# Differential attention scores: crosswise stacked queries for the mixed products and 64-row pairs for the high-by-high products

## The chip, the cores and the metric

The kernel runs on one core of one Trainium2 chip. The metric is the device time of one execution in microseconds. Before the change it is 1485.94 us, the median of three runs (1484.71 to 1486.96).

## What is computed

A trunk of two layers over 1024 tokens of width 1024. Layer 0 is a differential attention: eight heads, each with two components of 64 query and key columns, whose two softmax maps are subtracted before they meet the values. Layer 1 is a latent attention (MLA), which the change doesn't touch. Cut to the part of layer 0:

```python
q = _rope(q.reshape(b, s, 2 * DA_HEADS, DA_QK_DIM), positions)   # 16 x 64
k = _rope(k.reshape(b, s, 2 * DA_HEADS, DA_QK_DIM), positions)
...
def block(qb):
    sc = jnp.einsum('bqhcd,bkhcd->bhcqk', qb, k, preferred_element_type=f32) * scale
    p = jax.nn.softmax(sc, axis=-1)
    p = p[:, :, 0] - lam * p[:, :, 1]
    return jnp.einsum('bhqk,bkhd->bqhd', p.astype(v.dtype), v)
```

All inputs are float32, and the result has to be near float32.

## The kernel before

**Products in two parts.** A float32 matrix is kept as a high part of type fp32r (rounded by a copy) and a low part (the rest). A projection is then three products, high by high, low by high, high by low (`mm3`, lines 173 to 175).

**Scores of layer 0.** A head's two components have 64 columns each, so a stack of high over low part fills the 128 rows of TensorE. `stack_k` (line 295) builds for each half of 512 keys a tile `ks` of 2 x 512 columns: component 0 has high in rows 0 to 63 and low in rows 64 to 127, component 1 has high in rows 64 to 127 and low in rows 0 to 63. `stack_q` (line 302) builds two tiles for each half of 512 queries: `qa` has the high part in both row halves, `qb` the low part in both. It takes two casts on ScalarE, two subtractions on GpSimd and four copies from one row half to the other by SyncE's DMA queue. A query tile of 128 then needs, for each component, `qa` and `qb` against the two key halves: four products of 128 rows and 512 columns, which give all four of high and low by high and low.

**A query tile** (`attn0`, from line 821). Eight heads have eight tiles of 128 queries. For each tile `scores(0)` fills one score bank (128 x 1024 in PSUM; there are two such banks), `softmax_part` takes its maximum on VectorE (L352) and its exponential on ScalarE (L354) into `e` in SBUF, `scores(1)` does the same with the second bank, where the exponential stays in place. VectorE's reciprocal (L864), a scale (L865) and L866 subtract the second map from the first, and L866 is the last to read the second bank.

**What lies between.** Behind a tile come the tails of the two tiles before it: `turn` transposes `e` by four products of 128 columns (L335), ScalarE casts them into `pth` (L337), VectorE makes `ptl` (L338); `pv` multiplies them with the values, 12 products of 256 columns at a time, and only in every second tile (an odd one, `t` = 1). `fill(i)` takes the next steps of `stream0`, the q, k and z projections of the next head, three products of 512 columns to a step; tables (`FILL0`, `FILL7` for the last head) say how many steps at each of six places.

**What sets the order.** The code states the work in the order given above; the framework's scheduler then orders each engine's instructions by its own estimate, so neighbours in the code needn't stay neighbours. Every engine runs its instructions in the order in which they stand, and waits by semaphores.

Of the kernel before, what the change touches and what calls it, by code (L numbers as in the profile page):

```python
# [11 lines left out]
F32 = mybir.dt.float32  # L12
F32R = mybir.dt.float32r
# [8 lines left out]
P = 128  # L22
D = 1024
T = 1024
NT = T // P
KT = D // P
HF = 512
# [9 lines left out]
    NVEC += _c  # L37
DEF = 9
DEF1 = 0
FILL0 = ((1, 2, 1, 1, 1, 0), (1, 1, 1, 1, 1, 1))  # L40
FILL1 = ((1, 0, 1, 0), (0, 1, 0, 0)) * 4
SPL1 = 2
Z_PRE = 8
# [5 lines left out]
OP1 = (12, 4)  # L49
LAST = [(((0, 1, 2, 3), 0, HF),), (((0, 1), 0, HF), ((2,), 0, HF), ((3,), 0, 256), ((3,), 256, HF))]  # L50
Z_LAST = 2
FILL7 = ((0, 1, 1, 1, 1, 1),) * 4
G_WAIT = 3
G1_AT = 7
VB = (2, 4)
# [18 lines left out]
def f32v(ap):  # L74
    return ap.bitcast(F32)
# [3 lines left out]
def trunk(ctx: ExitStack, tc: tile.TileContext, A, out):  # L79
    nc = tc.nc  # L80
    SP, PE, V, S, G = nc.sync, nc.tensor, nc.vector, nc.scalar, nc.gpsimd
# [220 lines left out]
    def stack_q(qa, qb, r):  # L302

        S.copy(qa[0:64, 0, :], r[0:64])
        S.copy(qa[64:128, 1, :], r[64:128])
        G.tensor_sub(qb[0:64, 0, :], r[0:64], f32v(qa[0:64, 0, :]))
        G.tensor_sub(qb[64:128, 1, :], r[64:128], f32v(qa[64:128, 1, :]))
        for t in (qa, qb):
            SP.dma_start(f32v(t[64:128, 0, :]), f32v(t[0:64, 0, :]))
            SP.dma_start(f32v(t[0:64, 1, :]), f32v(t[64:128, 1, :]))  # L310

    def store_v(l, sp, acc, tt, fh):
        v = sp.tile([P, 2, HF], F32R, name="v_hl", tag="vst", bufs=VB[l])
        S.copy(v[:, 0, :], acc)
        V.tensor_sub(v[:, 1, :], acc, f32v(v[:, 0, :]))  # L315
# [33 lines left out]
    def softmax_part(ap_, s_ps, zs):  # L349

        nm = sm.tile([P, 1], F32, name="nm")
        V.reduce_max(nm, s_ps, axis=AX.X, negate=True)  # L352
        e = ap_.tile([P, T], F32, name="e", tag="e", bufs=3) if ap_ else s_ps
        S.activation(e, s_ps, AF.Exp, bias=nm, scale=1.0, accum_out=zs)  # L354
        return e

    def bcast_rows(sp, y, tag, bufs):
# [258 lines left out]
    KS, QS, GZ = {}, {}, {}  # L616
# [13 lines left out]
    def q_done(h):  # L630
        def f(acc, half):
            fin = rope(wp, acc, half, SC0)

            def g():
                qa = a0a.tile([P, 2, HF], F32R, name="qa", tag="qs", bufs=4)
                qb = a0a.tile([P, 2, HF], F32R, name="qb", tag="qs", bufs=4)
                stack_q(qa, qb, fin())
                QS.setdefault(h, [None, None])[half] = qa, qb

            side.add(*[None] * DEF, g)  # L640
        return f
# [34 lines left out]
    a0a = pool(st2a, "a0a")  # L676
# [29 lines left out]
    a0b = pool(st2b, "a0b")  # L706
# [80 lines left out]
    tails, hooks = [None, None], []  # L787
# [16 lines left out]
    def after_scores(fill, n):  # L804

        prev, last = tails
        if last:
            last.turn(0)
        fill(n)
        if prev:  # L810
            prev.pv(0)
        fill(n + 1)
        new = hooks[:]
        if prev:
            prev.pv(1)
        fill(n + 2)
        for f in new:
            hooks.remove(f)
            f()

    def attn0(h, fills, extra=None, late=None):

        def close(half, o_, zz):
            if late and half == 1:
                ctx_["late"] = late(o_, zz)
                return
            o = a0b.tile([P, HF], F32, name="o", tag="o", bufs=2)
            sq = a0b.tile([P, HF], F32, name="osq", tag="osq", bufs=4)
            head_out(o_, o, sq)
            subln(o, sq, zz, half, h, None)  # L830

        ctx_ = dict(pool=a0b, l=0, h=h, open=lambda half: None, close=close)
        for qp in range(4):
            half = qp // 2
            if qp % 2 == 0:
                zz = sm.tile([P, 4], F32, name="zz")
            for t in range(2):
                ti = (qp * 2 + t) % 4
                ql = slice(ti * P, (ti + 1) * P)
                zs = [zz[:, ti : ti + 1], sm.tile([P, 1], F32, name="z1")]  # L840
                es = []
                fl = fills(qp * 2 + t)

                def fill(i):
                    if fl[i]:
                        stream0.step(fl[i])

                def scores(c):
                    s_ps = bank("sc", "s", [P, T])
                    qa, qb = QS[h][half]  # L850
                    for src, fst in ((qa, True), (qb, False)):
                        for kc in range(2):
                            PE.matmul(s_ps[:, kc * HF : (kc + 1) * HF], src[:, c, ql], KS[h][kc][:, c, :], start=fst, stop=not fst)  # L853
# [10 lines left out]
                V.reciprocal(z1, z1)  # L864
                V.tensor_scalar(z1, z1, z0, neglam[:, 0:1], op0=ALU.mult, op1=ALU.mult)  # L865
                V.scalar_tensor_tensor(out=e0, in0=e1, scalar=z1[:, 0:1], in1=e0, op0=ALU.mult, op1=ALU.add)  # L866
                fill(2)
                after_scores(fill, 3)
# [12 lines left out]
    def load_ot(l, dst, src):  # L881
# [580 lines left out]
```

## Time and profile before

| what | value |
|---|---|
| median of three runs | 1485.94 us |
| profiled execution | 1489.61 us |
| its span | 1487.8 us |
| mean granted TensorE clock | 0.986 |
| TensorE products (PE) | 7424, all in the form 128*128 |
| maxima of 128 x 1024 (L352), both layers | 192, 1219 ns each |
| transposes (L335), both layers | 1024, 275 ns each, overlapping |

The profiled execution is 3.7 us above the median, so a sum made on it is carried over to the median as a difference. A product's duration in the profile runs from its start to its modelled end and overlaps with the next, so what a stream of them costs is read from start to start. "PE" is the product, "PEld" the load of its weights. In a row of waits the three numbers are the total in us, how often, and the longest.

### The profile page before, as it was taken

What the parts mean: (1) busy time and instruction counts of PE and PEld (TensorE: products, weight loads), DVE (VectorE), ACT (ScalarE), POOL (GpSimd) and SP (SyncE); (2) the same over time, 40 slices, a digit from 0 to 9 for tenths busy, and PEclk for the clock granted to TensorE, in tenths of its full rate; (3) what the DMA queues carried; (4) which work ended last, traced back from release to release, by engine and by line L of the source; (5) the groups of instructions that cost most, each with busy time, mean ns of one, the idle gap of its engine ahead of it and who ended that gap; (6) DMA issues with size and microseconds to landing.
All of it is one profiled execution on the core that took longest, in us unless ns stands there. A gap on an engine that the chain in (4) does not pass through costs nothing.

```text
span 1487.8 us, 20422 instructions
## 1 busy us (share of the span) xinstructions
PE 1411.2 (95%) x7424; PEld 1173.4 (79%) x7424; DVE 863.0 (58%) x1294; ACT 707.0 (48%) x1248; POOL 608.2 (41%) x472
## 2 busy tenths in 40 slices
PE   4999799999999999998899999999999999999997
PEld 3777688888888888877787778777888888888885
DVE  7655767776676767677435535224545555555455
ACT  4432365656565655666343332124445454455442
POOL 3426163636454544545561254213122041233582
PEclk9999899999999999998999999999999999999998
DMA  8885923233332323243453126467223232252453
GB/s 270 268 244 166 307 58 92 79 92 79 89 83 86 79 82 94 67 136 112 164 176 120 43 61 198 137 178 218 74 67 95 66 116 62 62 180 80 156 164 140
DMA packets 119829, 187.46 MB, mean 126 GB/s; under 512 B 17328, under 2 KB 54320, under 8 KB 119728
## 3 DMA queue, kind: packets, MB, share of 16 engines
q1 hardware_dynamic: 119728, 186.16, 41.7%
q8 instruction: 58, 0.95, 0.3%
q14 instruction: 43, 0.35, 0.1%
HBM read 124.82 MB, written 37.70 MB: 109 GB/s over the span
## 4 chain that ended last, share of the span: by engine, by line
PE 68%; DMA 13%; DVE 7%; POOL 5%; issue 3%; ACT 3%; SPq 2%; POOLq 0%; ACTq 0%; DVEq 0%
PE s L1284 9%; PE acc L175 8%; PE acc L174 8%; PE acc L173 8%; PE s L853 8%; PE tr L335 7%; PE pv L174 4%; PE pv L173 4%; PE pv L175 4%; DMA vS<-v_hl 3%; PE oacc L175 2%; PE oacc L174 2%; PE oacc L173 2%; DMA wor<-in_w_out 1%; POOL wol L911 1%
## 5 line engine op out<-in xcount | busy, mean ns | idle before, releaser
L352 DVE TENSOR_REDUCE nm<-s 128x1 f32<-128x1024 f32 x192 | 233.8, 1219 | 72.4 <-PE s L853 65.5
L337 ACT CAST pth<-tr 128x512 fp32r<-128x512 f32 x256 | 150.4, 587 | 255.0 <-PE tr L335 253.6
L338 DVE TENSOR_TENSOR ptl<-tr,pth 128x512 fp32r<-128x512 f32 x256 | 176.2, 688 | 151.5 <-ACT pth L337 150.3
L200 POOL TENSOR_TENSOR wl<-wraw,wh 128x512 fp32r<-128x512 f32 (+2 forms) x94 | 116.2, 1238 | 276.8 <-ACT wh L199 244.0
L335 PE MATMUL tr<-ident,e 128*128 128x128 f32 x1024 | 156.0, 275 | 4.0 <-DVE ptl L338 3.6
L335 PEld LDWEIGHTS tr<-ident,e 128*128 128x128 f32 x1024 | 121.9, 141 | 46.0 <-DVE ptl L338 17.6
L354 ACT ACTIVATE e<-s,nm 128x1024 f32<-128x1024 f32 x128 | 143.4, 1120 | 22.2 <-DVE nm L352 21.6
L173 PE MATMUL acc<-h0h,wh 128*128 128x512 f32 x360 | 149.6, 416 | 1.5 <-DVE v_hl L315 1.5
L173 PE MATMUL pv<-pth,vt 128*128 128x256 f32 x512 | 147.9, 289 | 1.4 <-ACT pth L337 1.4
L174 PE MATMUL pv<-ptl,vt 128*128 128x256 f32 x512 | 146.7, 286 | 0.0
L175 PE MATMUL pv<-pth,vt 128*128 128x256 f32 x512 | 145.9, 285 | 0.0
L175 PE MATMUL acc<-h0h,wl 128*128 128x512 f32 x360 | 142.5, 396 | 0.9 <-POOL wl L200 0.9
L174 PE MATMUL acc<-h0l,wh 128*128 128x512 f32 x360 | 142.1, 395 | 0.0
L911 POOL TENSOR_TENSOR wol<-wor,woh 128x512 fp32r<-128x512 f32 x64 | 86.2, 1366 | 75.2 <-ACT woh L910 74.8
L173 PEld LDWEIGHTS pv<-pth,vt 128*128 128x128 f32 x512 | 98.7, 193 | 5.2 <-ACT pth L337 2.4
L174 PEld LDWEIGHTS pv<-ptl,vt 128*128 128x128 f32 x512 | 98.6, 193 | 2.9
L175 PEld LDWEIGHTS pv<-pth,vt 128*128 128x128 f32 x512 | 98.6, 193 | 0.0
L853 PE MATMUL s<-ks,qa 128*128 128x512 f32 x256 | 85.6, 417 | 13.4 <-ACT e L354 5.7
L716 POOL TENSOR_TENSOR o<-o,bc_s 128x512 f32<-128x512 f32 x30 | 46.5, 1549 | 121.2 <-DVE o L1254 94.6
L199 ACT CAST wh<-wraw 128x512 fp32r<-128x512 f32 (+2 forms) x94 | 55.2, 589 | 84.1 <-PE acc L174 39.2
L287 POOL TENSOR_TENSOR rp_sw<-rp_sw,sinT 128x512 f32<-128x512 f32 x42 | 55.0, 1309 | 76.2 <-DMA rp_sw<-rp_raw 53.4
L866 DVE SCALAR_TENSOR_TENSOR e<-s,z,e 128x1024 f32<-128x1024 f32 x64 | 82.0, 1281 | 1.5
(491 smaller groups left out, 3300.9 us busy)
## 6 DMA issues: line engine op xcount, KB each, us to landing
wraw<-in_w_s SPq DMA_DIRECT2D x76, 256.0 KB, 2.9
ada<-in_ada_ss SPq DMA_DIRECT2D x32, 512.0 KB, 5.0
vS<-v_hl SPq DMA_DIRECT2D x32, 512.0 KB, 5.5
vt<-vS SPq DMA_DIRECT2D x32, 512.0 KB, 3.7
wor<-in_w_out SPq DMA_DIRECT2D x64, 256.0 KB, 3.5
rp_sw<-rp_raw SPq DMA_DIRECT2D x168, 64.0 KB, 2.0
bc_s<-bc_d SPq DMA_DIRECT2D x34, 256.0 KB, 3.7
ada<-in_ada_g SPq DMA_DIRECT2D x16, 512.0 KB, 5.3
```

The costliest lines, as they stand in the source:

```text
L173: PE.matmul(psum, ah, bh, start=first, stop=False)
L174: PE.matmul(psum, ah, bl, start=False, stop=False)
L175: PE.matmul(psum, al, bh, start=False, stop=last)
L200: (V if pair_of else G).tensor_sub(l_[:, :n], raw[:, :n], f32v(h_[:, :n]))
L335: PE.transpose(tr[:, j, :], p[:, kt * P : (kt + 1) * P], ident)
L337: S.copy(pth[kh][:, :, dst], tr)
L338: V.tensor_sub(ptl[kh][:, :, dst], tr, f32v(pth[kh][:, :, dst]))
L352: V.reduce_max(nm, s_ps, axis=AX.X, negate=True)
L354: S.activation(e, s_ps, AF.Exp, bias=nm, scale=1.0, accum_out=zs)
L853: PE.matmul(s_ps[:, kc * HF : (kc + 1) * HF], src[:, c, ql], KS[h][kc][:, c, :], start=fst, stop=not fst)
L911: G.tensor_sub(lo, raw, f32v(hi))
L1284: PE.matmul(s_ps[:, kc * HF : (kc + 1) * HF], lhs, rhs(kc), start=i == 0, stop=i == 4)
```

## The change

The mixed terms and the high-by-high terms are separated. `stack_x` replaces `stack_q`: one cast makes `qn`, the high part of both components as they lie (component 0 in rows 0 to 63, component 1 in rows 64 to 127); `qx` has crosswise, for component 0, the low part in rows 0 to 63 and the high part in rows 64 to 127, and for component 1 the high part in rows 0 to 63 and the low part in rows 64 to 127. A product of `qx` with `ks` over 128 rows is low by high plus high by low. The high-by-high term is a product of `qn` and `ks` over the 64 rows of its component. Low by low is no longer computed. A query tile has two products of 128 rows and two of 64 rows for each component, eight in all as before. SyncE makes two copies per query half where it made four. Both score banks are now filled together: the four mixed products, then the four of 64 rows, alternating between the components, and only then the two softmax parts. The places of the fills and the two tables are arranged anew, with 12 steps for two tiles of `FILL0` and 5 for a tile of `FILL7` as before.

```diff
-FILL0 = ((1, 2, 1, 1, 1, 0), (1, 1, 1, 1, 1, 1))
+FILL0 = ((1, 2, 1, 1, 1, 0), (1, 2, 1, 1, 1, 0))
...
-FILL7 = ((0, 1, 1, 1, 1, 1),) * 4
+FILL7 = ((1, 1, 1, 1, 1, 0),) * 4
...
+    def stack_x(qn, qx, r):
+
+        S.copy(qn, r)
+        G.tensor_sub(qx[0:64, 0, :], r[0:64], f32v(qn[0:64]))
+        G.tensor_sub(qx[64:128, 1, :], r[64:128], f32v(qn[64:128]))
+        SP.dma_start(f32v(qx[64:128, 0, :]), f32v(qn[0:64]))
+        SP.dma_start(f32v(qx[0:64, 1, :]), f32v(qn[64:128]))
...
-                qa = a0a.tile([P, 2, HF], F32R, name="qa", tag="qs", bufs=4)
-                qb = a0a.tile([P, 2, HF], F32R, name="qb", tag="qs", bufs=4)
-                stack_q(qa, qb, fin())
+                qn = a0a.tile([P, HF], F32R, name="qn", tag="qn", bufs=3)
+                qx = a0a.tile([P, 2, HF], F32R, name="qx", tag="qx", bufs=3)
+                stack_x(qn, qx, fin())
...
-                def scores(c):
-                    s_ps = bank("sc", "s", [P, T])
-                    qa, qb = QS[h][half]
-                    for src, fst in ((qa, True), (qb, False)):
-                        for kc in range(2):
-                            PE.matmul(s_ps[:, kc * HF : (kc + 1) * HF], src[:, c, ql], KS[h][kc][:, c, :], start=fst, stop=not fst)
-                    es.append(softmax_part(None if c else a0b, s_ps, zs[c]))
-
-                scores(0)
-                fill(0)
                 if tails[0]:
                     tails[0].turn(1)
+                fill(0)
+                qn, qx = QS[h][half]
+                sp = [bank("sc", f"s{c}", [P, T]) for c in range(2)]
+                for c in range(2):
+                    for kc in range(2):
+                        PE.matmul(sp[c][:, kc * HF : (kc + 1) * HF], qx[:, c, ql], KS[h][kc][:, c, :], start=True, stop=False)
+                for kc in range(2):
+                    for c in range(2):
+                        r = slice(c * 64, c * 64 + 64)
+                        PE.matmul(sp[c][:, kc * HF : (kc + 1) * HF], qn[r, ql], KS[h][kc][r, c, :], start=False, stop=True)
+                nms = [row_max(sp[0])]
+                e0 = row_exp(a0b.tile([P, T], F32, name="e", tag="e", bufs=3), sp[0], nms[0], zs[0])
                 fill(1)
-                scores(1)
-                e0, e1 = es
+                prev, last = tails
+                if last:
+                    last.turn(0)
+                nms.append(row_max(sp[1]))
+                e1 = row_exp(sp[1], sp[1], nms[1], zs[1])
```

Behind that, `pv(0)`, `pv(1)` and the hooks come with fills between them as before. `row_max` and `row_exp` are the two halves of `softmax_part`.

What the scheduler makes of it, at three places in the fifth head (its stream is that of most heads). The first place is TensorE's queue in an even tile of 128 queries. `s` are score banks, `acc` the stream's accumulator, `ks`, `qa`, `qb` and `qn`, `qx` the stacks. Before, the tile's two banks are filled apart from each other:

```order
L853 MATMUL s_4310<-ks_3783,qa_4020 128x512 [waits Activation_49]
L853 MATMUL s_4310<-ks_3877,qa_4020 128x512
L853 MATMUL s_4310<-ks_3783,qb_4021 128x512
L853 MATMUL s_4310<-ks_3877,qb_4021 128x512
L173 MATMUL acc_4256<-h0h4_0_118,wh_4159 128x512
L174 MATMUL acc_4256<-h0l4_0_119,wh_4159 128x512
L175 MATMUL acc_4256<-h0h4_0_118,wl_4160 128x512 [waits Pool_49]
```

Now, in the same tile (L867 are the mixed products over 128 rows, L871 those over 64 rows, `s0` and `s1` the two components):

```order
L867 MATMUL s0_4290<-ks_3759,qx_3997 128x512 [waits Activation_49]
L867 MATMUL s0_4290<-ks_3858,qx_3997 128x512
L867 MATMUL s1_4291<-ks_3759,qx_3997 128x512 [waits DVE_49]
L867 MATMUL s1_4291<-ks_3858,qx_3997 128x512
L871 MATMUL s0_4290<-ks_3759,qn_3996 128x512
L871 MATMUL s1_4291<-ks_3759,qn_3996 128x512
L871 MATMUL s0_4290<-ks_3858,qn_3996 128x512
L871 MATMUL s1_4291<-ks_3858,qn_3996 128x512
```

The second bank's products moved up behind the first's, and the four of 64 rows alternate between the components. 28 of the 64 tiles stand so.

The second place is TensorE's queue in the odd tile ahead of it. Before, stream products and transposes (`tr`) stand ahead of the second bank's four:

```order
L853 MATMUL s_4219<-ks_3877,qb_4021 128x512
L173 MATMUL acc_4163<-h0h6_1_128,wh_3902 128x512
L174 MATMUL acc_4163<-h0l6_1_129,wh_3902 128x512
L175 MATMUL acc_4163<-h0h6_1_128,wl_3903 128x512
L335 MATMUL tr_4231<-ident_79,e_4062 128x128 [waits DVE_49]
L335 MATMUL tr_4231<-ident_79,e_4062 128x128 x3
L173 MATMUL acc_4163<-h0h7_1_132,wh_3902 128x512
L174 MATMUL acc_4163<-h0l7_1_133,wh_3902 128x512
L175 MATMUL acc_4163<-h0h7_1_132,wl_3903 128x512
L853 MATMUL s_4245<-ks_3783,qa_4020 128x512 [waits DVE_49]
```

Now:

```order
L867 MATMUL s0_4199<-ks_3759,qx_3997 128x512 [waits Activation_49]
L867 MATMUL s0_4199<-ks_3858,qx_3997 128x512
L871 MATMUL s0_4199<-ks_3759,qn_3996 128x512
L871 MATMUL s0_4199<-ks_3858,qn_3996 128x512
L173 MATMUL acc_4134<-h0h7_1_132,wh_3872 128x512
L174 MATMUL acc_4134<-h0l7_1_133,wh_3872 128x512
L867 MATMUL s1_4200<-ks_3759,qx_3997 128x512 [waits DVE_49]
L867 MATMUL s1_4200<-ks_3858,qx_3997 128x512
L871 MATMUL s1_4200<-ks_3759,qn_3996 128x512
L871 MATMUL s1_4200<-ks_3858,qn_3996 128x512
```

Here the 64-row products of the two components stand apart, as in 22 tiles; in the other 14 tiles one of component 0 stands ahead of component 1's mixed products, and the other between component 1's two.

The third place is VectorE's queue for the even tile. `nm` are the maxima, `ptl` the low parts of the transposes, `z` the sums; the first row still belongs to the tile ahead. Before:

```order
L866 SCALAR_TENSOR_TENSOR e_4226<-s_4245,z1_4218,e_4226 128x1024 [waits DVE_49]
L352 TENSOR_REDUCE nm_4315<-s_4310 128x1 [waits PE_49]
L338 TENSOR_TENSOR ptl_4263<-tr_4322,pth_4261 128x4x128 [waits Activation_49]
L352 TENSOR_REDUCE nm_4340<-s_4335 128x1 [waits PE_49]
L338 TENSOR_TENSOR ptl_4262<-tr_4359,pth_4260 128x4x128 [waits Activation_49]
```

Now:

```order
L359 TENSOR_REDUCE nm_4300<-s0_4290 128x1 [waits PE_49]
L359 TENSOR_REDUCE nm_4317<-s1_4291 128x1 [waits PE_49]
L346 TENSOR_TENSOR ptl_4226<-tr_4310,pth_4224 128x4x128 [waits Activation_49]
L881 RECIPROCAL z1_4279<-z1_4279 128x1 [waits Activation_49]
L882 TENSOR_SCALAR z1_4279<-z1_4279,zz_4113,neglam_96 128x1 [waits DVE_49]
L883 SCALAR_TENSOR_TENSOR e_4302<-s1_4291,z1_4279,e_4302 128x1024 [waits DVE_49]
```

The two maxima stand next to each other, with no transpose's `ptl` between them.

More of the change, by code (lines that the diff above doesn't have):

```diff
@@ L347, in alloc_pt, with row_max, row_exp, softmax_part @@
         return pth, ptl
-    def softmax_part(ap_, s_ps, zs):
+    def row_max(s_ps):
         nm = sm.tile([P, 1], F32, name="nm")
         V.reduce_max(nm, s_ps, axis=AX.X, negate=True)
-        e = ap_.tile([P, T], F32, name="e", tag="e", bufs=3) if ap_ else s_ps
+        return nm
+    def row_exp(e, s_ps, nm, zs):
         S.activation(e, s_ps, AF.Exp, bias=nm, scale=1.0, accum_out=zs)
         return e
+    def softmax_part(ap_, s_ps, zs):
+        return row_exp(ap_.tile([P, T], F32, name="e", tag="e", bufs=3), s_ps, row_max(s_ps), zs)
     def bcast_rows(sp, y, tag, bufs):
@@ L634, in g @@
             def g():
-                qa = a0a.tile([P, 2, HF], F32R, name="qa", tag="qs", bufs=4)
-                qb = a0a.tile([P, 2, HF], F32R, name="qb", tag="qs", bufs=4)
-                stack_q(qa, qb, fin())
-                QS.setdefault(h, [None, None])[half] = qa, qb
+                qn = a0a.tile([P, HF], F32R, name="qn", tag="qn", bufs=3)
+                qx = a0a.tile([P, 2, HF], F32R, name="qx", tag="qx", bufs=3)
+                stack_x(qn, qx, fin())
+                QS.setdefault(h, [None, None])[half] = qn, qx
             side.add(*[None] * DEF, g)
@@ L840, in attn0 @@
                 zs = [zz[:, ti : ti + 1], sm.tile([P, 1], F32, name="z1")]
-                es = []
                 fl = fills(qp * 2 + t)
@@ L867, in attn0 @@
                 fill(2)
-                after_scores(fill, 3)
+                if prev:
+                    prev.pv(0)
+                fill(3)
+                new = hooks[:]
+                if prev:
+                    prev.pv(1)
+                fill(4)
+                for f in new:
+                    hooks.remove(f)
+                    f()
+                fill(5)
                 side.tick()
```

## The prediction

> **What bounds the kernel now.** I read the page's busy shares first, then the stage table, then the waits of TensorE in the stage, then single instructions. The change touches the score products of layer 0, so the first row to find is the one that says where they lie.
>
> ```profile
> span 1487.8 us, 20422 instructions
> PE 1411.2 (95%) x7424; PEld 1173.4 (79%) x7424; DVE 863.0 (58%) x1294; ACT 707.0 (48%) x1248; POOL 608.2 (41%) x472
> L853 PE MATMUL s<-ks,qa x256: 387/393/796, 164.2 to 705.4; 128*128 128x512 f32 x128
> 296.00:362.00 66.00, 65.72 (x371) 55.94 (x370) 44.52 (x67) 40.53 (x71) 33.78 (x27) 1.00 0.31 82
> 560.00:626.00 66.00, 65.71 (x363) 55.17 (x362) 45.27 (x69) 39.80 (x70) 35.35 (x28) 1.00 0.32 85
> ```
>
> The scores run from 164.2 to 705.4 us. In that stage's steady windows (columns: time, length, then busy us of PE, PEld, DVE, ACT, POOL, then granted clock, DMA share, GB/s) TensorE is busy 65.7 of 66 us at full clock, while VectorE has 44.5 and ScalarE 40.5. So the stage is bound by TensorE. Its waits, over all of 164 to 710 us:
>
> ```profile
> PE s L853 <- ACT e L354: 5.7, 3, 4.4
> PE s L853 <- DVE v_hl L315: 3.6, 1, 3.6
> PE tr L335 <- DVE ptl L338: 2.7, 2, 1.6
> PE s L853 <- DMA wor<-in_w_out: 2.2, 1, 2.2
> PE s L853 <- DVE e L866: 2.0, 7, 0.3
> PE pv L173 <- ACT pth L337: 1.4, 2, 0.8
> ```
>
> That is 17.6 us in 546, and 11.5 of them are the first waits and one DMA near the end (5.7, 3.6, 2.2). The 6.1 us of the other three rows are waits on VectorE and ScalarE that more work on TensorE would swallow. What one product costs is read from the chain and the timeline:
>
> ```profile
> 302.33 0.91 PE s L853 x4
> 303.92 0.44 PE tr L335 x4
> 301.47 0.39 PE L173 MATMUL acc<-h0h,wh 128*128 128x512 f32 x1
> 301.71 0.40 PE L174 MATMUL acc<-h0l,wh 128*128 128x512 f32 x1
> 301.94 0.39 PE L175 MATMUL acc<-h0h,wl 128*128 128x512 f32 x1
> 302.17 0.61 PE L853 MATMUL s<-ks,qa 128*128 128x512 f32 x2
> ...
> 303.53 0.39 PE L175 MATMUL acc<-h0h,wl 128*128 128x512 f32 x1
> 303.76 0.60 PE L335 MATMUL tr<-ident,e 128*128 128x128 f32 x4
> ```
>
> Four score products take 0.91 us of the chain: **a step of 0.228 us** each. A product itself lasts 0.39 us, so 0.39 - 0.228 = **0.165 us of tail** runs beside the next one. Four transposes of 128 columns, each with a weight load of its own, take 0.44: a weight load needs at most 0.11 us.
>
> **What the change removes on TensorE.** Before, each of 64 query tiles has 8 products over 128 rows: 512 steps. After, it has 4 of those (mixed terms) and 4 over 64 rows (high by high, rows 0 to 63 for component 0, rows 64 to 127 for component 1). The 64-row product still streams 512 columns, so alone it takes a step like any other, 0.228; what can be saved is the overlap of two neighbours on different rows. The instruction order tells how many such neighbours there are. In 28 tiles the four stand as 0 1 0 1; in 14 tiles one 0 stands alone and then 1 0 1; in 22 tiles they stand as 0 0 and 1 1 apart from each other, where nothing can overlap. If both of a pair ran at once, that would save 2 steps in each of the 28 and 1 step in each of the 14: 70 x 0.228 = 16.0 us, the upper bound. But each product needs its own weight load, and at 0.11 us each the second of a pair starts 0.11 late. 0 1 0 1 then takes 0.456 + 0.11 = 0.567 in place of 0.912 (saves 0.345), 1 0 1 takes 0.456 in place of 0.684 (saves 0.228): 28 x 0.345 + 14 x 0.228 = 9.7 + 3.2 = **12.9 us**. The lower bound is 0, no overlap at all; I take 12.9, since the rows of transposes show weight loads at that rate. [...] No row of this trace has such a pair.
>
> **What the change adds on TensorE.** Every one of the 7424 products in the trace is 128*128. The new ones are 64*128, so the array goes over from one form to the other and back: twice in each of the 28 tiles, four times in most others. In the instruction order that is **204 changes of form**. Their price is in no row of the trace. It isn't below 0, since no product starts earlier than a step behind the one ahead. For the other end I take the place where the array really ran empty:
>
> ```profile
> 604.87 1.28 DVE L866 SCALAR_TENSOR_TENSOR e<-s,z,e 128x1024 f32<-128x1024 f32 x1
> 605.52 0.40 PE L175 MATMUL acc<-h0h,wl 128*128 128x512 f32 x1
> 606.20 0.73 PE L853 MATMUL s<-ks,qa 128*128 128x512 f32 x2 [0.29 <-DVE e L866]
> 606.77 0.63 PE L853 MATMUL s<-ks,qb 128*128 128x512 f32 x2
> ```
>
> From the restart at 606.20 to the third product at 606.77 are 0.57 us where two steps are 0.456: 0.11 for a weight load that nothing covers. So if a change of form lets the array run empty, it costs the tail of 0.165, and at most 0.165 + 0.11 = 0.275 when the load waits too. Between 0 and 0.275 I take **the tail, 0.165**: it is the row nearest to "the old form must be out before the new one goes in". 204 x 0.165 = 33.7 us (full price 56.1). Not all of it is on the path. In 22 tiles, nearly all odd ones, the change back stands right ahead of the product that waits for VectorE, so it costs 22 x 0.165 = 3.6 less, and the 6.1 us of waits above go. **24.0 us** stay (44.0 at the full price: 56.1 - 6.0 - 6.1).
>
> [...]
>
> **The wait that the new order tightens.** Both score banks are now filled together, and the bank of component 1 is free only after L866 of the tile before. The durations of that chain:
>
> ```profile
> L352 DVE TENSOR_REDUCE nm<-s 128x1 f32<-128x1024 f32 x192 | 233.8, 1219 | 72.4 <-PE s L853 65.5 <-PE s L1284 6.5
> L354 ACT ACTIVATE e<-s,nm 128x1024 f32<-128x1024 f32 x128 | 143.4, 1120 | 22.2 <-DVE nm L352 21.6
> L354 ACT ACTIVATE s<-s,nm 128x1024 f32<-128x1024 f32 x64 | 70.0, 1094 | 7.7 <-DVE nm L352 7.7
> L354 ACT ACTIVATION_READ_ACCUMULATOR e<-s,nm 128x1 f32 x128 | 25.3, 198 | 0.0
> L337 ACT CAST pth<-tr 128x512 fp32r<-128x512 f32 x256 | 150.4, 587 | 255.0 <-PE tr L335 253.6
> L864 DVE RECIPROCAL z<-z 128x1 f32<-128x1 f32 x64 | 10.3, 161 | 18.3 <-ACT s L354 18.1
> L865 DVE TENSOR_SCALAR z<-z,zz,neglam 128x1 f32<-128x1 f32 x64 | 17.4, 271 | 2.8 <-ACT e L354 1.0
> L866 DVE SCALAR_TENSOR_TENSOR e<-s,z,e 128x1024 f32<-128x1024 f32 x64 | 82.0, 1281 | 1.5
> ```
>
> From the first product of component 1 in an even tile: the rest of the scores 1.02 (0.456 + 0.567), tail 0.17, first maximum 1.22, exponential with its sum 1.32, the cast of the transposes that stands between 0.59, second exponential 1.29, reciprocal and scale 0.43, L866 1.28: 7.3 us. Behind that product TensorE has, up to the same product of the odd tile: 1.02 + 6 stream steps x 0.684 + 8 transposes x 0.11 + 3 steps of the odd tile's component 0 = 1.02 + 4.10 + 0.88 + 0.68 = 6.7 us. So an odd tile would wait up to 0.6 us; queued behind are the rest of that tile's scores, its stream steps, transposes and output products, all of TensorE's row. In 13 of the 32 odd tiles statistics products fill the gap, and in eight others two to four stream products were put ahead of the waiting one. So between 0 and 19 x 0.6 = 11 us, and nothing if the form changes delay TensorE anyway: 3 changes x 0.165 = 0.5 us is nearly the whole wait. With my price I cost it at 0.
>
> **The other edits.**
>
> ```profile
> 299.48 0.61 ACT L304 CAST qa<-rp_r 64x512 fp32r<-64x512 f32 x1
> 300.11 0.62 ACT L305 CAST qa<-rp_r 64x512 fp32r<-64x512 f32 x1
> 300.11 0.50 SPq L309 DMA_DIRECT2D qa<-qa  x1
> ```
>
> ScalarE's two casts per query half become one copy (16 instructions of 0.6 us fewer), SyncE issues 32 fewer copies of q at 0.5 us, VectorE's rows are the same but for their order. All of it lies beside a TensorE that is busy 65.7 of 66 us; if that cover went, the casts would be 16 x 0.6 = 10 us at most, but none of the waits above is for q. The fill tables still give 12 stream steps per two tiles. 0 us.
>
> **Sum.** -12.9 + 24.0 + 0 = +11.1 us on the profiled execution of 1489.6 (span 1487.8), so 1500.7 there; it is 3.7 above the median of 1485.9, and against that median the time is **1497.0 us**.
>
> **The rivals.** *The change of form is free (the other side).* If the array takes the new form behind the old without running empty, only the saving is left: 1485.9 - 12.9 = 1473.0. For it: the transposes of L335, another kind of product, follow the stream products at the ordinary step (303.53 to 303.76), without a gap. Against it: they keep 128*128. It decides where 182 paid changes (204 less 22) cost the saving and the waits, 12.9 + 6.1 us: below 0.10 us each the change is faster. Chance 0.37. *Pairs don't overlap*, so the change doesn't do what it says: nothing saved, 24.0 paid, 1509.9; or, with free changes, 1485.9. For it: no row shows two products at once. Chance 0.08. *The wait for the second bank takes the place of the gain*: free changes of form, 11 us of waits, 1485.9 - 12.9 + 11 = 1484.0; for it speaks the chain above, against it that the order already moves work into the gap. Chance 0.07. *The full price*: -12.9 + 44.0 = +31.1, 1517.0; it is the upper half of my forecast's own case, as nothing tells its price better than the two ends.
>
> **How the numbers follow.** The forecast's case, that the array empties at each change at a price between tail and full price, has 0.48, and 1497.0 is its likelier end. The range must take in the free case and the full price: 1470 (the free case with full overlap, 1485.9 - 16.0) to 1519 (the full price, and 2 us of the bank's wait). About 0.2% (3 us) is what a measurement of this kernel can tell from no change. Faster by more: 0.37 and 0.02 of the bank's case, 0.39; within it: the other 0.05 of that and 0.03 for serial pairs with free changes, 0.08; slower: 0.48 and 0.05 for serial pairs that pay, 0.53.
>
> **What would show it.** The step from a 128*128 product to a 64*128 product and back in the timeline: 0.39 or more says the array empties, 0.23 that it doesn't. Two 64*128 products of different components that start 0.11 us or less apart say that pairs overlap; 0.23 that they don't. A row "PE s <- DVE e" of 11 us or more would show the bank's wait. I am wrong altogether if the stage grows or shrinks where no score product stands.

## The result, and the profile after

The changed kernel takes **1520.91 us** (median of four runs, 1520.12 to 1521.92), against 1485.49 us for the kernel before (four runs, 1484.71 to 1486.96). The ratio is 1.0238, 95% interval 1.022 to 1.0255: 35.4 us slower. The prediction was 1497.0 us, with a range from 1470 to 1519.

The page of the profiled execution (1520.12 us), with the two groups of score products of layer 0 from the views of their lines (count, shortest/median/longest in ns, first and last start), and the windows view over the steady middle of the stage:

```profile
span 1518.3 us, 20259 instructions
PE 1438.0 (95%) x7424; PEld 1150.8 (76%) x7424; DVE 879.0 (58%) x1294; ACT 689.7 (45%) x1232; POOL 610.1 (40%) x472
L867 PE MATMUL s<-ks,qx x256: 387/393/796, 163.7 to 737.3; 128*128 128x512 f32 x128
L871 PE MATMUL s<-ks,qn x256: 388/493/793, 164.7 to 738.0; 64*128 64x512 f32 x128
200.00:650.00 450.00, 440.13 (x2339) 339.58 (x2338) 298.58 (x438) 236.41 (x426) 217.79 (x171) 0.98 0.26 72
```

The score stage lasts 574.3 us (163.7 to 738.0) where it was 541.7 (164.2 to 705.9): **32.6 us more**. The spans of the two profiled executions differ by 30.5 us (1518.3 less 1487.8), so all of that difference lies here. (The medians are further apart, 35.4, because the profiled execution of before, 1489.61 us, took 4.1 more than its median and that of the changed kernel 0.8 less.) In the 450 us of the window TensorE starts 2339 products. The kernel before starts more, at full clock (the third number from the end):

```profile
200.00:650.00 450.00, 448.03 (x2502) 378.49 (x2502) 310.40 (x470) 267.75 (x469) 236.47 (x185) 1.00 0.31 84
```

So there are three things to find: time in which TensorE is busy but gets less done, about 8 us more of idle time, and a clock that is not always granted in full. The waits of TensorE from 160 to 738 us (total, times, longest):

```profile
PE s L867 <- DVE e L883: 11.6, 6, 2.2
PE s L867 <- ACT e L364: 3.7, 2, 2.9
PE s L867 <- issue: 2.9, 1, 2.9
PE pv L173 <- ACT pth L345: 0.7, 1, 0.7
```

These are 18.9 us, against 17.6 before. The sum is nearly the same, but its largest row is new. L883 is the subtraction that was L866, and instead of seven waits of at most 0.3 us there are six of some 2 us.

**The price of the form**, of going over from 128-row to 64-row products and back, can be read from single rows of TensorE's timeline (start, duration of the group, idle time ahead of it in brackets). Three runs of 64-row products are shown: four in the order 0 1 0 1 of the components, two of one component, and a single one followed by 1 0 1.

```profile
309.22 1.07 PE L867 MATMUL s<-ks,qx 128*128 128x512 f32 x4
310.22 0.73 PE L871 MATMUL s<-ks,qn 64*128 64x512 f32 x4
310.88 0.50 PE L173 MATMUL acc<-h0h,wh 128*128 128x512 f32 x1
311.21 0.39 PE L174 MATMUL acc<-h0l,wh 128*128 128x512 f32 x1
...
316.04 0.61 PE L867 MATMUL s<-ks,qx 128*128 128x512 f32 x2
316.58 0.73 PE L871 MATMUL s<-ks,qn 64*128 64x512 f32 x2
317.24 0.50 PE L173 MATMUL acc<-h0h,wh 128*128 128x512 f32 x1
317.57 0.39 PE L174 MATMUL acc<-h0l,wh 128*128 128x512 f32 x1
...
298.88 0.63 PE L867 MATMUL s<-ks,qx 128*128 128x512 f32 x2
299.44 0.50 PE L871 MATMUL s<-ks,qn 64*128 64x512 f32 x1
299.87 0.73 PE L867 MATMUL s<-ks,qx 128*128 128x512 f32 x2
300.53 0.73 PE L871 MATMUL s<-ks,qn 64*128 64x512 f32 x3
301.19 0.50 PE L173 MATMUL acc<-h0h,wh 128*128 128x512 f32 x1
301.53 0.39 PE L174 MATMUL acc<-h0l,wh 128*128 128x512 f32 x1
```

Count a run from the end of the last ordinary step ahead of it to one step (0.228) before the start of the second ordinary product behind it. That way the first ordinary product's own delay is in the run. The four: from 309.22 + 4 x 0.228 = 310.13 to 311.21 - 0.228 = 310.98, so 0.85 us. The two: from 316.04 + 0.456 = 316.50 to 317.57 - 0.228 = 317.34, so 0.84 us. **Four products take as long as two**, so the pairs run side by side in full, with their weight loads. What is left over, 0.85 - 0.456 = 0.39, belongs to two changes of form: **0.20 us for each change**. By the same count a single product takes 0.64 us (its follower of 0.39 us starts at 299.87 + 0.73 - 0.39 = 300.21), and 1 0 1 takes 0.86.

Against ordinary steps of 0.228 a run of four costs -0.06 us, one of three +0.18, one of two +0.39 and a single one +0.41. The order has 28, 14, 42 and 18 of them (102 runs, 204 changes): -1.7 + 2.5 + 16.4 + 7.4 = **+24.6 us**. A row of two, which used to cost 0.456, is now nearly twice as long, and there are 42 of those.

**The new wait** in one place, on ScalarE, GpSimd, VectorE and TensorE in order of time:

```profile
350.33 0.21 ACT L364 ACTIVATION_READ_ACCUMULATOR s<-s,nm 128x1 f32 x1
350.86 1.29 POOL L287 TENSOR_TENSOR rp_sw<-rp_sw,sinT 128x512 f32<-128x512 f32 x1 [1.89 <-DMA rp_sw<-rp_raw]
352.19 0.69 DVE L290 TENSOR_TENSOR rp_r<-rp_r,rp_sw 128x512 f32<-128x512 f32 x1 [2.03 <-POOL rp_sw L287]
352.80 0.16 DVE L881 RECIPROCAL z<-z 128x1 f32<-128x1 f32 x1
353.30 1.28 DVE L883 SCALAR_TENSOR_TENSOR e<-s,z,e 128x1024 f32<-128x1024 f32 x1
354.64 0.73 PE L867 MATMUL s<-ks,qx 128*128 128x512 f32 x2 [1.83 <-DVE e L883]
```

The second softmax part is ready at 350.54 (350.33 + 0.21), so the reciprocal L881 could start there. But ahead of L881 in VectorE's queue stands L290, the addition of the next head's rope, which waits 2.03 us for GpSimd's L287, and that waited for a DMA; L881 starts behind L290, at 352.80. The subtraction comes 2.3 us late, and with it the second score bank. TensorE's own row for it shows 1.83 us. There are six such waits in the eight heads.

The addition stood ahead of a reciprocal before, too, but there it has no wait (VectorE's timeline of before):

```profile
343.84 0.68 DVE L290 TENSOR_TENSOR rp_r<-rp_r,rp_sw 128x512 f32<-128x512 f32 x1
344.44 0.16 DVE L864 RECIPROCAL z<-z 128x1 f32<-128x1 f32 x1
```

So what is new is not an addition ahead of the reciprocal, but one that has to wait some 2 us there for its operand. All waits of VectorE for it come to 18.8 us (20 times, at most 2.4) where they were 6.2 (eight times, at most 0.8).

**The clock.** Behind such a wait something more follows; the timeline of TensorE around the one that ends at 427.69, and the windows view over the same stretch:

```profile
425.09 0.73 PE L871 MATMUL s<-ks,qn 64*128 64x512 f32 x2
427.69 0.73 PE L867 MATMUL s<-ks,qx 128*128 128x512 f32 x2 [1.88 <-DVE e L883]
...
430.46 0.63 PE L173 MATMUL acc<-h0h,wh 128*128 128x512 f32 x1
430.89 0.63 PE L174 MATMUL acc<-h0l,wh 128*128 128x512 f32 x1
```

```profile
424.00:428.20 4.20, 2.33 (x9) 1.18 (x8) 2.88 (x6) 1.71 (x3) 2.67 (x3) 1.00 0.12 46
428.20:432.00 3.80, 3.80 (x11) 2.59 (x11) 2.30 (x3) 1.22 (x2) 1.58 (x2) 0.60 0.00 0
```

Ordinary products start 0.43 us apart (430.46 to 430.89) instead of 0.228: the clock granted in that window is 0.60. By its records it is at half speed for 3.4 us from 428.95 on, and 3.0 of these lie in the window. The records of the granted clock hold 37.4 us at half speed in the score stage of this execution, and 23.8 us in that of before, where all of it lies at the stage's start and end. The 13.6 us between them are four stretches between 200 and 650 us, each behind a wait for the subtraction; half of that, 6.8 us, is time lost.

Three terms, then: forms +24.6, waits +1.3 (18.9 less 17.6), half clock +6.8. Their sum is 32.7; the stage grew by 32.6. That they meet so closely is partly luck: the stage now also holds ten more of the 512-column products, some 2 us that no term counts, so the terms are good to 2 or 3 us.

### The profile page after: what moved, and what is told of

The parts are those of the page before. It is cut to its first block, busy times and chain, and to the rows that moved or that the text cites. A ratio compares the mean times of both kernels' runs of the same rounds, so it can differ in the third digit from the quotient of the medians.

```text
span 1518.3 us, 20259 instructions
## 1 busy us (share of the span) xinstructions
PE 1438.0 (95%) x7424; PEld 1150.8 (76%) x7424; DVE 879.0 (58%) x1294; ACT 689.7 (45%) x1232; POOL 610.1 (40%) x472
## 5 line engine op out<-in xcount | busy, mean ns | idle before, releaser
L364 ACT ACTIVATE e<-s,nm 128x1024 f32<-128x1024 f32 x128 | 143.2, 1119 | 107.4 <-DVE nm L359 106.8
L173 PE MATMUL acc<-h0h,wh 128*128 128x512 f32 x360 | 160.1, 445 | 0.8 <-DVE v_hl L323 0.8
L343 PEld LDWEIGHTS tr<-ident,e 128*128 128x128 f32 x1024 | 124.4, 143 | 44.3 <-DVE ptl L346 15.2
L174 PE MATMUL acc<-h0l,wh 128*128 128x512 f32 x360 | 145.3, 404 | 0.0
L867 PE MATMUL s<-ks,qx 128*128 128x512 f32 x256 | 79.8, 411 | 18.1 <-DVE e L883 11.6
L173 PEld LDWEIGHTS acc<-h0h,wh 128*128 128x128 f32 x360 | 69.3, 192 | 28.1 <-issue 20.8
L286 POOL TENSOR_TENSOR rp_r<-rp_raw,cosT 128x512 f32<-128x512 f32 x42 | 56.5, 1346 | 78.4 <-ACT rp_raw L281 40.8
```

Of the source, the lines that this page charges most:

```text
L173: PE.matmul(psum, ah, bh, start=first, stop=False)
L174: PE.matmul(psum, ah, bl, start=False, stop=False)
L286: G.tensor_mul(r, raw, cosT[:, cs])
L343: PE.transpose(tr[:, j, :], p[:, kt * P : (kt + 1) * P], ident)
L867: PE.matmul(sp[c][:, kc * HF : (kc + 1) * HF], qx[:, c, ql], KS[h][kc][:, c, :], start=True, stop=False)
```

## The experiments

Theory F says that the changes of form make the loss, at 0.20 us each with pairs that overlap in full. Theory W says that it is the new order, with its waits. Times are medians; differences go to the median of the kernel before on the same chip, and a ratio, which isn't the quotient of the two medians, can differ from it by 0.2% (1489.45 us for the first four, 1487.65 for the next four, 1488.01 for e9 and e10, 1489.84 for e11).

**e1, one run per tile**: each tile's 64-row products are held together behind the mixed ones, so that there are 128 changes instead of 204.

```diff
-  PE.matmul(sp[c][...], qn[r, ql], KS[h][kc][r, c, :], start=False, stop=True)
+  with tc.issue_after(mm.ins):
+      mm = PE.matmul(sp[c][...], qn[r, ql], KS[h][kc][r, c, :], start=False, stop=True)
```

> The changed kernel, but the four 64-row products of every tile are issued one behind the other and behind both components' mixed products: 64 runs in the order 0 1 0 1 and 128 changes of form in place of 204. Theory F (each change of form costs about 0.20 us, a pair overlaps in full): a run 0 1 0 1 takes 0.85 us where its four products took 0.91 before, so 64 x -0.06 = -4 us, plus the some 8 us by which waits and order lengthen the stage now, plus up to 8 us where component 1's products can no longer wait behind 64-row products: 1490 to 1498 us. Theory W (the wait for the second score bank and the new order are the cost): unchanged or longer, 1520 us or more.

Measured 1506.23 us, +16.8, ratio 1.0116 (1.0095 to 1.0137). Its waits for the subtraction grew to 15.2 us, nine times, and those for ScalarE's L364 to 6.5. Neither expectation was met: the gain is 18.6 us on the changed kernel, less than theory F has. Fewer changes help, but more waits take part of it back.

**e2, no 64-row form**: the changed kernel with the high-by-high products over all 128 rows.

```diff
-  r = slice(c * 64, c * 64 + 64)
-  PE.matmul(sp[c][...], qn[r, ql], KS[h][kc][r, c, :], start=False, stop=True)
+  PE.matmul(sp[c][...], qn[:, ql], KS[h][kc][:, c, :], start=False, stop=True)
```

> The changed kernel, but the four high-by-high products run over all 128 rows of qn and of the stacked keys, so there is no 64-row form and nothing to pair; the terms that these rows add are not those of the reference. Theory F: the 24.7 us of runs go, the 8 us of waits and order stay: 1493 us. Theory W: 1520 us. If pairs had overlapped without changes being dear, it would be slower than the changed kernel by 16 us: 1537.

Measured 1499.84 us, +10.4, ratio 1.0079 (1.0059 to 1.01). The changed kernel is 35.4 above its before and this one 10.4, so **25.0 us** go with the form; the rows above gave 24.6. The two traces differ in more than the form, though: e2's waits in the stage are 3.7 us longer (22.6 against 18.9) and its half clock costs 6.8 us less (23.8 us against 37.4). Of the 23.4 us between the two stages (574.3 and 550.9) that leaves 20 for the form, so it is worth 20 to 25. The other 10 us are there without a single change of form. Six waits for the subtraction (L882 in this kernel), 13.1 us in all, are new against before, and this row of VectorE's waits shows the addition again, about as in the changed kernel:

```profile
DVE rp_r L290 <- POOL rp_sw L287: 20.4, 20, 2.5
```

**e3, before's order**: the components one behind the other as before, with the new stacks; 128 runs of two, 256 changes.

```diff
+  for kc in range(2):
+      PE.matmul(s_ps[...], qx[:, c, ql], KS[h][kc][:, c, :], start=True, stop=False)
+  for kc in range(2):
+      PE.matmul(s_ps[...], qn[r, ql], KS[h][kc][r, c, :], start=False, stop=True)
```

> The kernel before, with its order (component 0's scores and softmax, then component 1's) and its fills, but with the new stacks: two mixed products and two 64-row products for each component, 128 runs of 0 0 or 1 1, 256 changes of form, nothing that can pair. Theory F: 128 x 0.39 = 50 us more than before: 1535 us. Theory W: the second bank is filled as late as before, so 1485 us.

Measured 1528.49 us, +39.0, ratio 1.0267 (1.0249 to 1.0285). By the rows above the changes cost 128 x 0.39 = 50; TensorE's waits in the stage fall from 17.6 to 6.6 us, which gives 11 back. No wait for the subtraction is among them: the new stacks alone, in the old order, don't bring it.

**e4, the form in layer 1**: the kernel before, with one product of layer 1's scores cut to 64 rows; 58 runs of two and 12 of one, 140 changes, no pairs. That product multiplies `qb` with the stacked rotary keys, and drops low by low.

```diff
-  (qb[:, c, ql], lambda kc: KP[kc]),
+  (qb[0:64, c, ql], lambda kc: KP[kc][0:64]),
```

> The kernel before, with layer 0 untouched; in layer 1 the product of the queries' low part with the stacked rotary keys runs over 64 rows (low by low is left out): 58 runs of two 64-row products and 12 of one, 140 changes of form, no pair, no change of order at a bank. Theory F: 58 x 0.39 + 12 x 0.41 = 27.5 us, less what waits in that stage swallow: 1508 to 1513 us. Theory W: 1485 us.

Measured 1514.37 us, +24.9, ratio 1.0168 (1.0146 to 1.019); 58 x 0.39 + 12 x 0.41 = 27.5 was expected, less what waits swallow. So the price holds in another stage with other neighbours: 24.9 / 140 = 0.18 for each change, with no saving in it.

**e5 to e8, the addition behind the subtraction.** Each takes a kernel above and queues the rope additions and the stacking that follows them behind the tile's last subtraction (e8 does it to the kernel before, as a control):

```diff
-            side.add(*[None] * DEF, g)
+            side.add(*[None] * DEF, late(g))
...
-  V.scalar_tensor_tensor(out=e0, in0=e1, scalar=z1[:, 0:1], in1=e0, ...)
+  stt[0] = V.scalar_tensor_tensor(out=e0, in0=e1, scalar=z1[:, 0:1], in1=e0, ...).ins
+  hold[0] = False
+  while pend:
+      with tc.issue_after(stt[0]):
+          pend.pop(0)()
```

`late(g)` keeps `g` in `pend` while a tile's scores are being written out, and else issues it behind `stt[0]`.

> The run with 128-row high-by-high products (as e2: their sums take in terms that the reference does not have) and one more edit: VectorE's rope additions and the stacking that follows them are queued behind a tile's last subtraction instead of ahead of it. No change of form, and the same number of 512-column steps as before. If the 10.4 us of e2 are waits of TensorE for a subtraction that stands behind a rope addition in VectorE's queue (6 waits, 13.1 us in its trace), those waits go, and the time falls to that of the kernel before, within -2 to +3 us. If they come from the order of the products or from the two scores' banks being filled and freed together, the time stays at +8 to +12 us.

> The run with all four 64-row products of a tile in one run (as e1: 64 runs of '0 1 0 1', 128 changes of form), and the rope additions queued behind the tile's last subtraction. By 0.20 us for each change and pairs that overlap in full, the products cost 64 x -0.06 = -4 us against before; e1's 16.8 us above before held 15.2 us of waits for the subtraction and 6.5 us for the row maximum's read. If the queue order makes those waits, the time comes to -4 to +5 us of before. If the waits belong to the one run itself (the first component's score is complete only near the end of the run, so that the softmax starts later in every tile), they stay, in some other row, and the time stays at +13 to +19 us.

> The changed kernel with the one edit of the rope additions' place in VectorE's queue. The order then holds 28 runs '0 1 0 1', 6 of '1 0 1', 59 of two products on the same rows and 8 single ones: 28 x -0.06 + 6 x 0.19 + 59 x 0.39 + 8 x 0.41 = +25.7 us against before, with nothing for waits. Changed kernel as measured: +35.4 us. If the queue order makes the remaining 10 us, this one comes to +23 to +28 us; if it does not, +33 to +38 us.

> The control: the kernel before with the same edit of VectorE's queue. In its trace the wait for a subtraction is 2.0 us in all, so both theories expect -2 to +2 us; a larger gain would say that the edit helps by itself and that e5 to e7 must be read against this run.

| run | as | us | to before | ratio (95%) | without this edit |
|---|---|---|---|---|---|
| e5 | e2 | 1478.01 | -9.6 | 0.9927 (0.9906 to 0.9948) | +10.4 |
| e6 | e1 | 1489.08 | +1.4 | 0.9998 (0.9986 to 1.0009) | +16.8 |
| e7 | changed kernel | 1502.68 | +15.0 | 1.0084 (1.006 to 1.0108) | +35.4 |
| e8 | before | 1487.02 | -0.6 | 0.999 (0.9972 to 1.0008) | 0 |

The one edit takes 20 us from e2 and from the changed kernel and 15 from e1, and nothing from before. e6 and e8 came out as expected, e5 and e7 about 8 us below the lower end of what I had expected. In e5 the addition stands behind the subtraction (timeline of VectorE and ScalarE, the same tile of the head), and TensorE's waits for the subtraction are down to one:

```profile
343.60 0.22 ACT L364 ACTIVATION_READ_ACCUMULATOR s<-s,nm 128x1 f32 x1
343.85 0.16 DVE L893 RECIPROCAL z<-z 128x1 f32<-128x1 f32 x1 [0.41 <-ACT s L364]
344.36 1.28 DVE L895 SCALAR_TENSOR_TENSOR e<-s,z,e 128x1024 f32<-128x1024 f32 x1
345.56 0.68 DVE L290 TENSOR_TENSOR rp_r<-rp_r,rp_sw 128x512 f32<-128x512 f32 x1
```

```profile
PE s L880 <- DVE e L895: 0.5, 1, 0.5
```

I had expected this edit to return 7 to 12 us in e5. It returned 20, because half clock went with the waits (windows view, 200 to 650 us, of e2 and of e5):

```profile
200.00:650.00 450.00, 436.95 (x2413) 370.22 (x2412) 306.88 (x452) 244.51 (x441) 227.09 (x178) 0.99 0.28 73
```

```profile
200.00:650.00 450.00, 449.74 (x2511) 380.55 (x2510) 321.01 (x472) 254.60 (x455) 233.65 (x181) 1.00 0.28 75
```

From 436.95 busy us to 449.74, and 98 products more. The stage went from 550.9 us to 530.9: 12.5 us of waits (22.6 to 10.1) and 8.5 us of half clock ((23.8 - 6.8) / 2) make 21.0. Of the 8.5 us, 5.1 lie between 200 and 650 us, behind waits for the subtraction; the other 3.4 lie at the stage's start and end. e7 less e5 is 24.7 us, near the 25.7 of the run counts in its expectation. Here too the traces differ in waits (7.0 us against 10.1) and in half clock (20.5 us against 6.8), which leaves some 23 of the 27.0 us between the stages for the form. e6's one run of four is -4 us by the same prices, yet it stays 11.1 us above e5: its waits are 7.5 us longer (17.6 against 10.1) and its half clock (23.8 us against 6.8) costs 8.5 us more, together the 16 us that are missing to within 1. What in the one run makes those waits I didn't try.

**e9, the old stacks in the new order**, to see whose the gain of e5 is: `qa` and `qb` as before, both banks filled together, the addition behind (the edit is shown against the changed kernel).

```diff
-  PE.matmul(sp[c][...], qx[:, c, ql], KS[h][kc][:, c, :], start=True, stop=False)
+  PE.matmul(sp[c][...], qa[:, c, ql], KS[h][kc][:, c, :], start=True, stop=False)
...
-  PE.matmul(sp[c][...], qn[r, ql], KS[h][kc][r, c, :], start=False, stop=True)
+  PE.matmul(sp[c][...], qb[:, c, ql], KS[h][kc][:, c, :], start=False, stop=True)
```

> The stacks of the kernel before (qa, qb; all eight products of a tile over 128 rows, the whole computation), issued in the changed kernel's order with both components' banks filled together, and the rope additions queued behind the tile's last subtraction. No change of form. If the 9.6 us that e5 gained on the kernel before come from this order (shorter waits at 165 to 175 us and fewer stretches of TensorE at half its clock: 6.8 us of them in the score stage of e5, 23.8 us in that of before), they are here too: 1476 to 1481 us. If they come from the smaller stacks (one DMA pair and one stack less for every half of a head), the time is that of the control, -2 to +2 us of before.

Measured 1484.16 us, -3.9, ratio 0.9978 (0.9965 to 0.9991): between the two expectations. The order keeps under half of the gain. The rest goes with the smaller stacks, at the stage's start (waits of TensorE from 160 to 200 us in e9, then the windows view there):

```profile
PE s L880 <- ACT e L364: 4.5, 1, 4.5
PE s L880 <- DVE v_hl L323: 3.9, 1, 3.9
```

```profile
160.00:200.00 40.00, 31.55 (x140) 24.76 (x139) 29.51 (x42) 16.47 (x30) 7.66 (x6) 0.83 0.62 203
```

The second row is one of before's first waits too (3.6 us there), and neither e5 nor e11 has it; behind it the clock is at half speed for 13.7 us, the longest such stretch of e9. In e5 the wait for ScalarE's L364 is there too, but shorter (2.9 us).

**e10, the order 0 0 1 1** in e6's run of four:

```diff
-  for kc in range(2):
-      for c in range(2):
+  for c in range(2):
+      for kc in range(2):
```

> e6 with the four 64-row products of a tile in the order 0 0 1 1 in place of 0 1 0 1; still 64 runs and 128 changes of form. If neighbours on different rows overlap in full, a run of 0 0 1 1 takes three steps (only the second and third overlap) where 0 1 0 1 takes two: 64 x 0.228 = 14.6 us above e6, +14 to +19 us of before. If products on different rows don't overlap, the time stays at e6's, -2 to +4 us of before.

Measured 1488.53 us, +0.5, ratio 1.0003 (0.9991 to 1.0015), e6's time within 1 us. By itself that reads as "no overlap", but the rows say the opposite (timeline of TensorE in e10):

```profile
306.27 0.73 PE L885 MATMUL s<-ks,qn 64*128 64x512 f32 x4
306.93 0.50 PE L173 MATMUL acc<-h0h,wh 128*128 128x512 f32 x1
307.26 0.39 PE L174 MATMUL acc<-h0l,wh 128*128 128x512 f32 x1
```

Four products in 0.66 us (306.27 to 306.93), as 0 1 0 1 (310.22 to 310.88) and as 0 0 alone (316.58 to 317.24) in the changed kernel. My test was wrong: it took for granted that the second 0 holds up the first 1 behind it. In e10's trace it doesn't; products on the other rows start ahead of the one that waits. The trace shows the passing itself: the products that complete a bank, which stand second and fourth of the four in the queue, are marked by an update of a semaphore, and in all 64 tiles the marked ones start third and fourth. So what was said of the kernel before, that every engine runs its instructions in the order in which they stand, holds for VectorE in the rows of the new wait (L881 behind L290), but not for e10's 64-row products of TensorE on different rows.

**e11, a version that beats both**: the changed kernel's `qx`, order and two DMAs, but no 64-row form. `qz` holds the high part of a component in its own 64 rows and zeros in the others (two buffers, zeroed once), so the high-by-high product runs over 128 rows; and the addition stands behind the subtraction. Low by low is left out, as in the changed kernel. (In the last line of the cut `qn` is the name under which the tile's `qz` is taken up.)

```diff
+    QZ = [a0a.tile([P, 2, HF], F32R, name="qz", tag=f"qz{i}", bufs=1) for i in range(2)]
+    for t_ in QZ:
+        G.memset(f32v(t_[64:128, 0, :]), 0.0)
+        G.memset(f32v(t_[0:64, 1, :]), 0.0)
...
+    def stack_z(qz, qx, r):
+
+        S.copy(qz[0:64, 0, :], r[0:64])
+        S.copy(qz[64:128, 1, :], r[64:128])
...
-  PE.matmul(sp[c][...], qn[r, ql], KS[h][kc][r, c, :], start=False, stop=True)
+  PE.matmul(sp[c][...], qn[:, c, ql], KS[h][kc][:, c, :], start=False, stop=True)
```

> The whole computation without a change of form: the changed kernel's crosswise stack qx, its order and its two DMAs for each half of a head, but the high-by-high products over 128 rows of a stack qz whose other 64 rows are zeros (written once into two buffers), and the rope additions queued behind the tile's last subtraction. ScalarE copies two halves of 64 rows in place of one of 128. If e5's 9.6 us belong to the order and the smaller stacks together (e9, with the old stacks, kept 3.9 of them), this one comes to 1476 to 1481 us, faster than both kernels. If two buffers for qz or the additional copies hold the stage's start, it comes to 1482 to 1486 us, as e9.

Measured **1475.99 us**, -13.9, ratio 0.9914 (0.9899 to 0.9928), faster than both kernels. The page's span, TensorE's longest waits for layer 0's scores and the windows view from 200 to 650 us:

```profile
span 1473.0 us, 20361 instructions
PE s L893 <- ACT e L373: 3.8, 2, 3.1
PE s L893 <- POOL o L754: 2.7, 1, 2.7
200.00:650.00 450.00, 449.53 (x2512) 380.63 (x2511) 320.62 (x474) 262.84 (x469) 234.03 (x181) 1.00 0.29 75
```

## Why the prediction was wrong, step by step

The direction held, and so did the core of the mechanism: a change of form costs time, and more than the pairs save. The size didn't: the forecast missed by 23.9 us, and the loss was 35.4 where the sum had 11.1. Three terms were wrong: the price of a change was too low, the waits that were to go came back as others, and the half clock wasn't in the sum.

- **Saving by pairs, 12.9: too small by 3.1.** I had the second of a pair start 0.11 late for its weight load. The rows show 0 1 0 1 as long as 0 0 (0.85 and 0.84 us), so the load runs beside too, and the upper bound of 16.0 holds. That a 64-row product alone takes a step of 0.228 was an estimate; a run of two takes 0.20 us more than a single one (0.84 and 0.64). In the changed kernel's trace the starts of 61 of the 70 pairs lie 3 to 4 ns apart, the others 0 to 5.
- **Price of a change, 0.165: mis-sized.** Measured 0.20, between the tail (0.165) and the full price (0.275) that I gave as ends. 204 x 0.20 is 40.8 where I had 33.7: 7.1 more. e4 gave 0.18 without pairs, and e2 against the changed kernel 20 to 25 us for price and saving together (40.8 - 16.0 = 24.8). Whether the array really runs empty, and so whether the old form must be out before the new one goes in, for which I took the tail, isn't shown; what the runs show is the 0.20. By my sign a step of 0.39 or more would say so and 0.23 the contrary; the step into the form is 0.32 (from 309.22 + 1.07 - 0.39 = 309.90 to 310.22), the one back behind a single product 0.43 (299.44 to 299.87), and the rest of the delay falls on the steps next to them.
- **3.6 off for changes ahead of a waiting product: not seen.** The runs' own prices add up to the whole loss without it.
- **Waits that go, 6.1: the step that failed in kind.** I took the waits of before for slack that more work on TensorE swallows. All but 0.7 of them did go, and so did some of the first ones, but the new order put a rope addition that still waits for GpSimd ahead of the subtraction on VectorE (11.6 us of waits), and the sum rose by 1.3: an error of 7.4. I read TensorE's queue in two places and VectorE's in one, a tile without an addition, and never asked where the additions stand. I had named a row of 11 us or more of "PE s <- DVE e" as the mark of the second bank's wait, and there is one of 11.6; but it isn't the chain of 7.3 us against 6.7 that I worked out. It goes in e5 and e7 with one edit of VectorE's order, and that chain is still there.
- **The clock: not in the sum.** 6.8 us lost at half speed behind the longer waits, in the stage where I had read a granted clock of 1.00.
- **The other edits, 0: they gain.** e9 and e11 differ in the stacks alone: two copies by SyncE for a query half in place of four, and `qx` and `qz` in place of `qa` and `qb`. They are 10 us apart. e11 is 2.8 us ahead at the stage's first score product and 8.0 at the 32nd, and stays so until the last head. So most of the gain is made at the stage's start, where the wait of 3.9 us goes, the other shrinks from 4.5 to 3.1, and the half clock falls from 13.7 to 3.4 us. (As a sum, 3.9 + 1.4 + 5.1 = 10.4, these are more than the 5.2 us that are gained there; which of them is worth how much stays open.) In the changed kernel this gain is in the sums of waits and clock above. I had costed the stacks' copies at nothing, since a busy TensorE covers them; at the start of the stage it waits. That it is the copies, and not another part of the stacks, no run separates.

11.1 + 3.6 + 7.1 + 7.4 + 6.8 - 3.1 = 32.9 us, and the stage grew by 32.6 (good to 2 or 3 us, as said). Of the rivals, the full price (1517.0) came nearest, yet for another reason: the price was 0.20, not 0.275, and the rest were waits and clock. The free change fell by every row above; serial pairs fell by the four products that take as long as two.

## What to carry to other kernels

Count the changes between 128-row and 64-row products in the scheduled order, not in the code: a pair saves one step, 0.228 us here, and a run costs two changes, 0.39 us, so two pairs in one run only just pay (-0.06 here), and a run without a pair doesn't (+0.39 and +0.41). Where an edit moves the work of one engine, look at the queue of the engine that frees its buffers, for a waiting instruction of another chain that now stands ahead. And price a wait of some 2 us on TensorE above its own length, for the clock that may follow it: here a stretch at half clock began behind 12 of 17 such waits.

## What the runs showed of the hardware

- **Half clock behind short waits.** From 200 to 650 us, the 13 traces have 17 waits of TensorE over 1 us, all of 2.0 to 2.6 us (from start to start, less a step). Behind 12 of them a stretch at half clock begins, from 0.3 us before the wait's end to 2.0 us after it, eleven of 3.4 us and one of 6.8. There is no other such stretch in that window of any trace. What spares the other five waits (2.0 to 2.4 us) no run shows. A stretch of 3.4 us costs half of that, 1.7: in one of them ordinary products start 0.43 us apart in place of 0.228.
- **64-row products pass one another in e10.** Two products on rows 0 to 63 stand ahead of two on rows 64 to 127, and the four take 0.66 us, as in alternating order; the first of the later two starts ahead of the second of the earlier two. So pairs need not alternate in the queue there.
- **A pair's second weight load costs no time that shows**: runs of two and of four differ by 0.01 us (0.84 and 0.85), though the four have twice the loads.
